# Instance norm over rows of 4096: two-pass statistics on both engines, with 4 MB tiles in six buffers and loads four ahead

## Chip, cores, metric

One core of one Trainium2 chip. The metric is device time in microseconds (us).

## The reference

```python
# x: (256, 256, 4096) float32, drawn from randn; eps = 1e-5
mean = np.mean(x, axis=2, keepdims=True)
var = np.var(x, axis=2, keepdims=True)
return ((x - mean) / np.sqrt(var + eps)).astype(np.float32)
```

That is 65,536 independent rows of 16 KB. 1.07 GB are read and 1.07 GB written.

## The kernel before

(Shortened.) Four rows on each of 128 partitions make a tile of 8 MB. Three such tiles fill the buffers. All transfers are issued by SP (the "queue" below), in one order.

```python
    P = 128
    K = 4
    BUFS = 3
    AHEAD = 2
    ...
    def load(i):
        x_tile = io.tile([P, K, d], mybir.dt.float32)
        nc.sync.dma_start(out=x_tile, in_=x_t[i])
        tiles[i] = x_tile

    def row(x_tile, r):
        ...
        for j in range(nsub):                       # nsub = 8, pieces of 512
            nc.vector.bn_stats(out=stats[:, j, :], in_=xr[:, r, j, :])
        nc.vector.bn_aggr(out=mv, in_=stats)
        nc.scalar.activation(out=rstd, in_=mv[:, 1:2], func=Sqrt, bias=eps_tile, scale=1.0)
        nc.vector.reciprocal(out=rstd, in_=rstd)
        nc.vector.scalar_tensor_tensor(out=nbias, ...)      # -mean * rstd
        nc.scalar.activation(out=x_tile[:, r, :], in_=x_tile[:, r, :],
                             func=Identity, bias=nbias, scale=rstd)

    def finish(i):
        x_tile = tiles.pop(i)
        for r in range(K):
            row(x_tile, r)
        nc.sync.dma_start(out=out_t[i], in_=x_tile)

    for i in range(AHEAD):
        load(i)
    for i in range(ntiles):
        finish(i)
        if i + AHEAD < ntiles:
            load(i + AHEAD)
```

## Time and profile before

| | before |
|---|---|
| time, median of 4 runs | 5018.83 us (5017.18 to 5019.74) |
| DMA engines' share on the data queue | 99.7% |
| VectorE, ScalarE busy | 53%, 42% |
| transfers, packet size | 256 of 8 MB, 65,536 B |
| instructions of VectorE, with waits | 5639 |

Read it from the DMA side. If the DMA share is at its top in every slice, busy shares of the compute engines say nothing about the time. What counts is GB/s, slice by slice (a page cuts the run into 40 equal slices), and the ends of the run. The lines are in the prediction.

### The profile page before, as it was taken

The numbers are of one execution on the slowest core, as the hardware profiler recorded it, in microseconds if no ns is written. First come the engines' busy times: TensorE is split into PE (matmuls) and PEld (weight loads), VectorE is DVE, ScalarE is ACT, GpSimd is POOL, SyncE is SP. The second block draws the span as 40 slices with busy tenths as digits, with TensorE's granted clock in tenths as the row PEclk, the third lists the DMA queues.
The fourth block names the chain that finished last, engine by engine and source line by source line (L and its number), as shares of the span: only waits on it lengthen the run. The fifth ranks groups of instructions, "written<-read, shape, count | busy, mean of one in ns | idle before, by whom it ended". The sixth has DMA issues, their size and how long they took to land.

```text
span 5018.0 us, 7844 instructions
## 1 busy us (share of the span) xinstructions
DVE 2667.3 (53%) x5633; ACT 2083.6 (42%) x1025; POOL 0.2 (0%) x4
## 2 busy tenths in 40 slices
DVE  5555455545555455554555545555455544555444
ACT  3444334443444334443344433444334443344433
POOL 0000000000000000000000000000000000000000
DMA  9999999999999999999999999999999999999998
GB/s 426 432 432 432 433 433 434 434 434 433 427 432 429 426 432 430 427 434 427 427 427 432 428 426 433 429 427 429 430 428 427 428 432 427 427 432 428 427 432 362
DMA packets 36925, 2148.00 MB, mean 428 GB/s; under 512 B 4096, under 2 KB 4096, under 8 KB 4096
## 3 DMA queue, kind: packets, MB, share of 16 engines
q1 hardware_dynamic: 36864, 2147.50, 99.7%
q14 instruction: 61, 0.50, 0.0%
HBM read 1073.74 MB, written 1073.74 MB: 428 GB/s over the span
## 4 chain that ended last, share of the span: by engine, by line
DVE 45%; another core or an unknown queue 43%; ACT 9%; DMA 1%; issue 1%; ACTq 0%
DVE stats L58 41%; ACT x_tile L76 9%; DVE mv L59 2%; DMA x_tile<-in_x_dram 1%; DVE rstd L67 1%; DVE nbias L68 1%; ACT rstd L60 1%; ACTq L60 0%
## 5 line engine op out<-in xcount | busy, mean ns | idle before, releaser
L58 DVE BATCH_NORM_STATS2 stats<-x_tile 128x6 f32<-128x512 f32 x4096 | 2506.3, 674 | 2228.2 <-DMA x_tile<-in_x_dram 2228.2
L76 ACT ACTIVATE x_tile<-x_tile,nbias,rstd 128x4096 f32<-128x4096 f32 x512 | 1945.7, 3800 | 403.5 <-DVE nbias L68 403.5
L60 ACT ACTIVATE rstd<-mv,eps_tile 128x1 f32<-128x1 f32 x512 | 148.8, 291 | 2508.5 <-DVE mv L59 2483.6
L59 DVE BATCH_NORM_AGGREGATE mv<-stats 128x2 f32<-128x48 f32 x512 | 183.7, 359 | 4.4
L67 DVE RECIPROCAL rstd<-rstd 128x1 f32<-128x1 f32 x512 | 74.8, 146 | 87.5 <-ACT rstd L60 87.3
L68 DVE SCALAR_TENSOR_TENSOR nbias<-mv,rstd 128x1 f32<-128x1 f32 x512 | 75.2, 147 | 4.3
L60 ACT ACT_TABLE_LOAD x1 | 1.3, 1283 | 0.7 <-PEq L112 0.7
L42 DVE MEMSET eps_tile<- 128x1 f32 x1 | 0.1, 59 | 0.8 <-PEq L112 0.8
L112 POOL MEMSET const-bfloat16-1.0<- 128x1 bf16 x1 | 0.1, 103 | 0.0
L112 POOL MEMSET const-uint8-127<- 128x1 uint8 x1 | 0.1, 102 | 0.0
L112 POOL MEMSET const-float32-0.0<- 128x1 f32 x1 | 0.1, 100 | 0.2 <-issue 0.2
L112 POOL MEMSET const-float32-1.0<- 128x1 f32 x1 | 0.1, 99 | 0.0
## 6 DMA issues: line engine op xcount, KB each, us to landing
x_tile<-in_x_dram SPq DMA_DIRECT2D x128, 52.3
out_dram<-x_tile SPq DMA_DIRECT2D x128, 33.3
```

The costliest lines, as they stand in the source:

```text
L42: nc.vector.memset(eps_tile, eps)
L58: nc.vector.bn_stats(out=stats[:, j, :], in_=xr[:, r, j, :])
L59: nc.vector.bn_aggr(out=mv, in_=stats)
L60: nc.scalar.activation(out=rstd, in_=mv[:, 1:2], func=mybir.ActivationFunctionType.Sqrt, bias=eps_tile, scale=1.0,)
L67: nc.vector.reciprocal(out=rstd, in_=rstd)
L68: nc.vector.scalar_tensor_tensor(out=nbias, in0=mv[:, 0:1], scalar=-1.0, in1=rstd, op0=mybir.AluOpType.mult, op1=mybir.AluOpType.mult,)
L76: nc.scalar.activation(out=x_tile[:, r, :], in_=x_tile[:, r, :], func=mybir.ActivationFunctionType.Identity, bias=nbias, scale=rstd,)
L112: nc = _bacc.Bacc("TRN2", target_bir_lowering=False, num_devices=1)
```

## The change

Its intent: fewer, longer instructions, shared by both engines, and smaller tiles of which more are in flight. The mean comes from a tensor_reduce in two stages, the squared deviations from a Square pass on ScalarE with an accumulator; one row is scaled by VectorE and the other by ScalarE. The same 24 MB of buffers hold six 4 MB tiles, and four loads are issued ahead. Instructions are kept in program order.

```diff
-    K = 4
-    BUFS = 3
-    AHEAD = 2
+    K = 2
+    BUFS = 6
+    AHEAD = 4
+    C = 64
...
-        for j in range(nsub):
-            nc.vector.bn_stats(out=stats[:, j, :], in_=xr[:, r, j, :])
-        nc.vector.bn_aggr(out=mv, in_=stats)
...
+        def mean(r):
+            row = x_tile[:, r, :].rearrange("p (c f) -> p c f", c=C)
+            keep(nc.vector.tensor_reduce(out=part[:, r, :], in_=row, axis=AX.X, op=ALU.add))
+            keep(nc.vector.tensor_reduce(out=nsum[:, c], in_=part[:, r, :], axis=AX.X, op=ALU.add, negate=True))
+            keep(nc.vector.tensor_scalar_mul(out=nmean[:, c], in0=nsum[:, c], scalar1=1.0 / d))
+        def square(r):
+            keep(nc.scalar.activation(out=junk, in_=x_tile[:, r, :], func=AF.Square,
+                                      bias=nmean[:, c], scale=1.0, accum_out=ss[:, c]))
+        def scales(c):          # Sqrt on ScalarE, reciprocal and nmean * rstd on VectorE
...
+        mean(0); square(0); mean(1)        # the loops of the diff, written out for k = 2
+        scales(row 0); square(1); scales(row 1)
+        apply_dve(1)                       # tensor_scalar on VectorE
+        apply_act(0)                       # Identity on ScalarE
...
     for i in range(AHEAD):
         load(i)
+    for i in range(last + 1):
+        compute(i)
+        store(i)
+        if i + AHEAD <= last:
             load(i + AHEAD)
```

(`junk` is a PSUM tile that takes the squares, which nobody reads.)

More of the change, by code (lines that the diff above doesn't have):

```diff
@@ L18 @@
     nc = tc.nc
+    keep = tc.keep_in_program_order
+    fp32 = mybir.dt.float32
+    AX = mybir.AxisListType
+    AF = mybir.ActivationFunctionType
+    ALU = mybir.AluOpType
     P = 128
-    K = 4
-    BUFS = 3
-    AHEAD = 2
+    K = 2
+    BUFS = 6
+    AHEAD = 4
+    C = 64
     x_flat = x.flatten_outer_dims()
@@ L26, with rows @@
     n, d = x_flat.shape
-    ntiles = n // (P * K)
-    assert n == ntiles * P * K
-    x_t = x_flat.rearrange("(t p k) d -> t p k d", p=P, k=K)
-    out_t = out_flat.rearrange("(t p k) d -> t p k d", p=P, k=K)
-    FMAX = nc.vector.BN_STATS_FMAX
-    nsub = d // FMAX
-    assert d == nsub * FMAX
+    assert n % (P * K) == 0 and d % C == 0
+    spans = [(t * P * K, K) for t in range(n // (P * K))]
+    last = len(spans) - 1
+    def rows(flat, span):
+        r0, k = span
+        return flat[r0 : r0 + P * k, :].rearrange("(p k) d -> p k d", k=k)
@@ L37 @@
     io = ctx.enter_context(tc.tile_pool(name="io", bufs=BUFS))
-    small = ctx.enter_context(tc.tile_pool(name="small", bufs=8))
+    small = ctx.enter_context(tc.tile_pool(name="small", bufs=4))
     singles = ctx.enter_context(tc.tile_pool(name="singles", bufs=1))
-    eps_tile = singles.tile([P, 1], mybir.dt.float32)
+    psum = ctx.enter_context(tc.tile_pool(name="psum", bufs=1, space=bass.MemoryType.PSUM))
+    eps_tile = singles.tile([P, 1], fp32)
     nc.vector.memset(eps_tile, eps)
+    junk = psum.tile([P, d], fp32)
@@ L44 @@
     tiles = {}
     def load(i):
-        x_tile = io.tile([P, K, d], mybir.dt.float32)
-        nc.sync.dma_start(out=x_tile, in_=x_t[i])
+        x_tile = io.tile([P, K, d], fp32)
+        keep(nc.sync.dma_start(out=x_tile[:, : spans[i][1], :], in_=rows(x_flat, spans[i])))
         tiles[i] = x_tile
-    def row(x_tile, r):
-        xr = x_tile.rearrange("p k (s f) -> p k s f", s=nsub)
-        stats = small.tile([P, nsub, 6], mybir.dt.float32)
-        mv = small.tile([P, 2], mybir.dt.float32)
-        rstd = small.tile([P, 1], mybir.dt.float32)
-        nbias = small.tile([P, 1], mybir.dt.float32)
-        for j in range(nsub):
-            nc.vector.bn_stats(out=stats[:, j, :], in_=xr[:, r, j, :])
-        nc.vector.bn_aggr(out=mv, in_=stats)
-        nc.scalar.activation(
-            out=rstd,
-            in_=mv[:, 1:2],
-            func=mybir.ActivationFunctionType.Sqrt,
-            bias=eps_tile,
-            scale=1.0,
-        )
-        nc.vector.reciprocal(out=rstd, in_=rstd)
-        nc.vector.scalar_tensor_tensor(
-            out=nbias,
-            in0=mv[:, 0:1],
-            scalar=-1.0,
-            in1=rstd,
-            op0=mybir.AluOpType.mult,
-            op1=mybir.AluOpType.mult,
-        )
-        nc.scalar.activation(
-            out=x_tile[:, r, :],
-            in_=x_tile[:, r, :],
-            func=mybir.ActivationFunctionType.Identity,
-            bias=nbias,
-            scale=rstd,
-        )
@@ L84, in finish, with compute, apply_dve, apply_act @@
-    def finish(i):
-        x_tile = tiles.pop(i)
-        for r in range(K):
-            row(x_tile, r)
-        nc.sync.dma_start(out=out_t[i], in_=x_tile)
+    def compute(i):
+        x_tile = tiles[i]
+        k = spans[i][1]
+        part = small.tile([P, K, C], fp32)
+        nsum = small.tile([P, K], fp32)
+        nmean = small.tile([P, K], fp32)
+        ss = small.tile([P, K], fp32)
+        std = small.tile([P, K], fp32)
+        rstd = small.tile([P, K], fp32)
+        nbias = small.tile([P, K], fp32)
+        def mean(r):
+            c = slice(r, r + 1)
+            row = x_tile[:, r, :].rearrange("p (c f) -> p c f", c=C)
[3 more added lines that the diff above has]
+        def square(r):
+            c = slice(r, r + 1)
+            keep(
+                nc.scalar.activation(
+                    out=junk, in_=x_tile[:, r, :], func=AF.Square, bias=nmean[:, c], scale=1.0, accum_out=ss[:, c]
+                )
+            )
+        def scales(c):
+            keep(nc.scalar.activation(out=std[:, c], in_=ss[:, c], func=AF.Sqrt, bias=eps_tile, scale=1.0 / d))
+            keep(nc.vector.reciprocal(out=rstd[:, c], in_=std[:, c]))
+            keep(nc.vector.tensor_mul(out=nbias[:, c], in0=nmean[:, c], in1=rstd[:, c]))
+        def apply_dve(r):
+            c = slice(r, r + 1)
+            row = x_tile[:, r, :]
+            keep(
+                nc.vector.tensor_scalar(
+                    out=row, in0=row, scalar1=rstd[:, c], scalar2=nbias[:, c], op0=ALU.mult, op1=ALU.add
+                )
+            )
+        def apply_act(r):
+            c = slice(r, r + 1)
+            row = x_tile[:, r, :]
+            keep(nc.scalar.activation(out=row, in_=row, func=AF.Identity, bias=nbias[:, c], scale=rstd[:, c]))
+        for r in range(k - 1):
+            mean(r)
+            square(r)
+        mean(k - 1)
+        scales(slice(0, k - 1))
+        square(k - 1)
+        for r in range(k - 2):
+            apply_dve(r)
+        scales(slice(k - 1, k))
+        apply_dve(k - 1)
+        apply_act(k - 2)
@@ L90, with store @@
+    def store(i):
+        keep(nc.sync.dma_start(out=rows(out_flat, spans[i]), in_=tiles.pop(i)[:, : spans[i][1], :]))
     for i in range(AHEAD):
         load(i)
-    for i in range(ntiles):
-        finish(i)
-        if i + AHEAD < ntiles:
+    for i in range(last + 1):
+        compute(i)
+        store(i)
+        if i + AHEAD <= last:
             load(i + AHEAD)
```

## The prediction

> **What bounds the kernel now.** I read the page from the top: busy shares, the slices, the queues.
>
> ```profile
> DVE 2667.3 (53%) x5633; ACT 2083.6 (42%) x1025; POOL 0.2 (0%) x4
> ...
> DMA  9999999999999999999999999999999999999998
> GB/s 426 432 432 432 433 433 434 434 434 433 427 432 429 426 432 430 427 434 427 427 427 432 428 426 433 429 427 429 430 428 427 428 432 427 427 432 428 427 432 362
> ...
> q1 hardware_dynamic: 36864, 2147.50, 99.7%
> ```
>
> Both compute engines are half idle; the DMA engines are full in every slice but the last. The bound is moving 2147.5 MB, and the change moves the same bytes. So the question is only what lies between 5018 us and the fastest these bytes can move. The trace's packet records give that: of the 32,768 data packets of 65,536 B, 95% took 2418 ns, which over 16 engines is 433.7 GB/s. At that pace the data takes 32768/16 x 2.418 = **4952 us**. All the change can win is 5018 - 4952 = 66 us, 1.3%. More than 2% faster is practically excluded.
>
> Where are these 66 us? Stages of the run (columns: stretch, length, busy time of the engines, clock, DMA share, GB/s), then the end:
>
> ```profile
> 200.00:1000.00 800.00, 435.61 (x919) 335.45 (x166) 0.00 (x0) 1.00 1.00 433
> 1000.00:2000.00 1000.00, 526.21 (x1112) 412.96 (x203) 0.00 (x0) 1.00 1.00 430
> 4000.00:4950.00 950.00, 510.65 (x1080) 398.91 (x197) 0.00 (x0) 1.00 1.00 429
> ```
>
> ```profile
> 4970.00:4978.00 8.00, 7.02 (x15) 0.31 (x2) 0.00 (x0) 1.00 0.93 401
> 4978.00:4986.00 8.00, 8.00 (x17) 7.00 (x3) 0.00 (x0) 1.00 0.25 107
> 4986.00:4996.40 10.40, 5.82 (x15) 8.96 (x5) 0.00 (x0) 1.00 0.01 6
> 4996.40:5016.00 19.60, 0.00 (x0) 0.00 (x0) 0.00 (x0) 1.00 0.99 428
> ```
>
> First: the rate falls from 433 to 429 GB/s after some 1000 us, though the DMA share stays 1.00. Over the 3950 us from 1000 to 4950 that is about 0.9%, 35 us. Second: before the last store the DMA stands nearly idle from 4978 to 4996.4 us (0.25 x 8 + 0.01 x 10.4 = 2 us of work in 18.4), because all other transfers are done and the last 8 MB tile is still being computed: **16 us**.
>
> For the first, the issuing queue:
>
> ```profile
> 4017.41 0.33 SPq L88 DMA_DIRECT2D out_dram<-x_tile  x1
> 4017.84 0.39 SPq L48 DMA_DIRECT2D x_tile<-in_x_dram  x1
> 4057.05 0.33 SPq L88 DMA_DIRECT2D out_dram<-x_tile  x1
> ```
>
> ```profile
> SPq L88 <- ACT x_tile L76: 3233.2, 128, 26.6
> SPq L88 <- DMA x_tile<-in_x_dram: 1631.0, 126, 20.5
> SPq L48 <- DMA out_dram<-x_tile: 22.3, 2, 12.2
> ```
>
> A store is issued every 39.2 us with the next load right behind it, and the queue waits for computation (L76), not for a free buffer. Lining the packets up end to start gives 16 chains, one per DMA engine (the records do not name the engine, so this is my reconstruction). Early on, a store waits 8 us in the queue before any engine starts it. From about 1150 us on, the engines that are ahead start it 1 to 2 us after its issue, while the slowest trails them by 12 us. The tile is complete only when the slowest has landed it; then come some 26 us of computation; then the store is issued, just as the fastest run dry. Before this point the slowest engine needed 38.90 us for a load and a store of 8 MB, the fast ones 38.65 to 38.70; afterwards all need 39.12. The excess appears as last packets of a transfer that take about 3 us instead of 2.418. So lookahead is just used up in this kernel.
>
> **What the Trainium skill says.** (1) "DMA: Bandwidth & Descriptors", section "Where 436 GB/s comes from": 16 ports give 435.2 GB/s. The packets' 433.7 agrees; no program change raises it. (2) "SBUF — State Buffer", section "The DMA setup-cost knee": about 2 us fixed cost per transfer. It doubles in number here, but the trace shows the next transfer's packets following with no gap, with 9 ns for the closing 4-byte packet, so in a filled queue it is hidden. (3) "VectorE: DVE Perf Modes", section "The perf-mode tier table": fp32 tensor_reduce runs at 1x (for 2048 elements its 1x row says 2293 ns), tensor_scalar at 2x (1227 ns). The kernel before has neither; its nearest, 674 ns for 512 elements of bn_stats, fits a 1x rate. (4) "ScalarE: Activation LUTs", section "What ACT_TABLE_LOAD costs": 280 + 0.833 ns per element, 93 ns more for a second per-row operand, so 3785 ns at 4096; the trace has 3800.
>
> **The change part by part.** Rows on which the costs rest:
>
> ```profile
> L58 DVE BATCH_NORM_STATS2 stats<-x_tile 128x6 f32<-128x512 f32 x4096 | 2506.3, 674 | 2228.2 <-DMA x_tile<-in_x_dram 2228.2
> L76 ACT ACTIVATE x_tile<-x_tile,nbias,rstd 128x4096 f32<-128x4096 f32 x512 | 1945.7, 3800 | 403.5 <-DVE nbias L68 403.5
> L60 ACT ACTIVATE rstd<-mv,eps_tile 128x1 f32<-128x1 f32 x512 | 148.8, 291 | 2508.5 <-DVE mv L59 2483.6
> ```
>
> *VectorE, per 4 MB tile (2 rows a partition).* Gone: 2 x (8 x 0.612 + 0.36 + 0.15 + 0.15) = 11.1 us. Added, as estimates scaled from the tier table's 2048-element figures: two reductions of 4096 elements at 4.43 us, each with a 64-element reduction and a small multiply (0.15 each, like the 146 ns reciprocal): 2 x 4.73 = 9.5; four tiny operations, 0.6; one tensor_scalar at 2x, 2.3. Sum 12.4 us, 3.2 ms in 256 tiles, 63%.
> *ScalarE, per tile.* Two Square passes with accumulator (3.8 plus perhaps 0.2), two Sqrt at 0.29, one apply at 3.8: 12.4 us against 8.2 before.
> *Path through a tile.* The engines now alternate: both means end at 9.5; the second Square at 13.6; Sqrt, reciprocal and multiply at 14.2; the VectorE apply at 16.5, when the next tile can begin; the ScalarE apply at 17.7. So a tile per **16.5 us**, latency **17.7 us**. The DMA needs 38.71/2 = 19.4 us for load and store of a tile. Compute fits, with 2.9 us to spare, though busier than now. All of it lies beside DMA work.
> *Lookahead.* Six 4 MB buffers hold the same 24 MB. When load i has landed, the filled queue holds three stores and three loads ahead of store i: 6 x 9.7 = 58 us. Store i is issued 18 us after landing, and load i+4 waits for store i-2, which lands some 31 us after, needed by 67. So the lag between engines may grow to about 35 us before anything runs dry; today 12 us is the end. At some 0.2 us per 16 MB over 128 such pairs the lag ends below 30 us. The loss of the 39.12 stage should not come.
> *Ends.* When the last load lands, three stores (29 us) are still queued, more than 17.7: the 16 us hole goes. At the start store 0 is ready at about 30 us, before four loads end at 41: no hole either.
> *Transfers.* 512 instead of 256, packets of 32 KB: if the pace per byte holds, 1.21 us each. Transfer ends double.
>
> Sum: the end is set by the slowest engine. 128 x 38.90 = 4979 us; its excess over 38.71 comes from fetch packets of 8 KB on the instruction queue (about 43 land on it, one per 128 instructions of VectorE), which halve with VectorE's instructions (5633 to some 2800): about -10. Doubled transfer ends: the other trailing engines, without such fetches, lost 0.1 us per pair against 38.71; doubled, another 0.1 x 128 = +13. Start and final receipt: 4, slow first packets: 4. Together **4990 us**, -0.6%.
>
> **Rivals.** (A) *Transfer ends cost by themselves*, and the 0.41 us per pair of the later stage is not lack of lookahead: then twice as many ends give 256 x 0.41 = 105 us instead of 52, hole gone: 5018 - 16 + 52 = 5054. For it: the excess sits in last packets, not in gaps. Against: under 1000 us the same ends cost a quarter of this. (B) *Compute becomes the bound*: 19.4 us per tile is passed if tensor_scalar ran at 1x and handovers cost 1 us, or if Square and Sqrt need different tables: a load is 1283 ns on the page, four per tile 5 us, so 21.6 us x 256 = 5500 us. Against: Identity and Sqrt already share one load; nothing in the trace settles Square. (C) *Everything is recovered*: 4952 + 8 = 4960. (D) *Nothing changes but the hole*: 5000.
>
> **Range and chances.** My sum and D lie at 4990 to 5000, C at 4960, A at 5054 with about one chance in eight. B has perhaps one in 25. Range 4960 to 5040; faster by over 2% 0.01, within 2% 0.95, slower 0.04.
>
> **What would show each step.** Right: GB/s near 433 to the end, with no fall after 1000 us; a last slice well over 362; no idle stretch before the last store; the queue waiting for landed stores rather than for computation; VectorE near 63%, ScalarE near 62%, one table load; reductions near 4.4 us, tensor_scalar near 2.3 us. Wrong: 32 KB packets over 1.21 us on average by more than 1% (A), or idle DMA in mid-run with tiles spaced over 19.4 us (B).

## More of the kernel before

```profile
q14 instruction: 61, 0.50, 0.0%
```

These are fetches of the program itself: 61 packets, half a megabyte, a share that rounds to nothing.

## The result

| | before | after |
|---|---|---|
| time, median of 4 runs | 5018.83 us | 4985.86 us (4984.90 to 4986.04) |
| ratio, 95% interval | | 0.9934 (0.9917 to 0.9952) |
| VectorE, ScalarE busy | 53%, 42% | 64%, 61% |
| transfers, packet size | 256, 65,536 B | 512, 32,768 B |

Ratios in this document are the mean time of one kernel's fast runs over the mean of the other's in the same rounds, so not quite the ratio of the quoted medians.

33 us were won, half of the 66 that there were. The page after, parts 1 to 3:

```profile
DVE 3189.2 (64%) x2817; ACT 3044.8 (61%) x1794; POOL 0.2 (0%) x4
...
GB/s 422 430 432 433 433 433 433 432 433 433 433 433 433 433 433 433 433 433 433 433 433 433 433 433 433 433 433 433 433 433 433 432 433 433 433 433 433 433 433 363
...
q1 hardware_dynamic: 73728, 2147.52, 99.9%
q14 instruction: 48, 0.39, 0.0%
```

Both compute engines work more, and the time is shorter. GB/s no longer falls in mid-run. The last slice is as poor as before, 363 against 362. The stages (columns as in the prediction: stretch, length, busy times, clock, DMA share, GB/s):

```profile
200.00:1000.00 800.00, 511.75 (x452) 487.32 (x287) 0.00 (x0) 1.00 1.00 433
1000.00:2000.00 1000.00, 643.97 (x567) 610.14 (x360) 0.00 (x0) 1.00 1.00 433
4000.00:4950.00 950.00, 607.92 (x540) 579.62 (x344) 0.00 (x0) 1.00 1.00 433
```

The waits of the queue have turned round. Before, a store waited for computation and hardly ever for a buffer. Now most of the waiting is a load that waits for a stored tile to land and leave its buffer free:

```profile
SPq L56 <- DMA out_dram<-x_tile: 2742.3, 246, 12.2
SPq L117 <- DVE x_tile L94: 1818.3, 256, 27.6
SPq L117 <- ACT x_tile L102: 212.5, 256, 1.0
```

The groups show what the new arithmetic costs:

```profile
L80 ACT ACTIVATE junk<-x_tile,nmean 128x4096 f32<-128x4096 f32 x512 | 1882.8, 3677 | 1887.4 <-DVE nmean L75 1887.4
L73 DVE TENSOR_REDUCE part<-x_tile 128x64 f32<-128x4096 f32 x512 | 2260.2, 4414 | 702.5 <-DMA x_tile<-in_x_dram 702.5
L102 ACT ACTIVATE x_tile<-x_tile,nbias,rstd 128x4096 f32<-128x4096 f32 x256 | 969.3, 3786 | 0.1
...
L94 DVE TENSOR_SCALAR x_tile<-x_tile,rstd,nbias 128x4096 f32<-128x4096 f32 x256 | 617.8, 2413 | 9.4
```

And the timeline of one tile, from its first reduction to the issue of its store:

```profile
2009.85 4.42 DVE L73 TENSOR_REDUCE part<-x_tile 128x64 f32<-128x4096 f32 x1 [2.71 <-DMA x_tile<-in_x_dram]
...
2027.36 0.34 SPq L117 DMA_DIRECT2D out_dram<-x_tile  x1
```

That is 17.5 us through a tile, and VectorE waits 2.71 us for the next load: compute keeps up.

Last, the end of the run:

```profile
4954.00:4962.00 8.00, 3.05 (x6) 7.79 (x4) 0.00 (x0) 1.00 0.17 74
4962.00:4972.60 10.60, 0.00 (x0) 0.00 (x0) 0.00 (x0) 1.00 0.93 399
4972.60:4983.00 10.40, 0.00 (x0) 0.00 (x0) 0.00 (x0) 1.00 0.07 28
```

In the last stretch a DMA share of 0.07 is one engine of 16: the packet records show a single packet in flight for 8.9 us, while 13 engines finished at 4972.6 and two more by 4973.9. In the first stretch three engines work and the rest wait for the last store, which is issued at 4961.97. So most engines still have a hole before the last store, of some 8 us, but the slowest one has none, and it sets the end. Before, all engines ended within 0.2 us of each other at 5016.7, because the last store made all of them start together.

### The profile page after: what moved, and what is told of

Same layout as the page of the kernel before. It is cut to its first block, busy times and chain, and to the rows that moved or that the text cites. A ratio compares the mean times of both kernels' runs of the same rounds, so it can differ in the third digit from the quotient of the medians.

```text
span 4983.9 us, 6181 instructions
## 1 busy us (share of the span) xinstructions
DVE 3189.2 (64%) x2817; ACT 3044.8 (61%) x1794; POOL 0.2 (0%) x4
## 2 busy tenths in 40 slices
DMA packets 73776, 2147.91 MB, mean 431 GB/s; under 512 B 8192, under 2 KB 8192, under 8 KB 8192
## 4 chain that ended last, share of the span: by engine, by line
DMA 63%; DVE 13%; another core or an unknown queue 12%; ACT 10%; issue 0%; SPq 0%; ACTq 0%
DMA x_tile<-in_x_dram 56%; DVE part L73 11%; DMA out_dram<-x_tile 8%; ACT junk L80 5%; ACT x_tile L102 5%; DVE nsum L74 1%; DVE nmean L75 0%; SPq L117 0%; DVE x_tile L94 0%; ACTq L156 0%; ACT std L86 0%; ACT L86 0%; DVE rstd L87 0%; DVE nbias L88 0%
## 5 line engine op out<-in xcount | busy, mean ns | idle before, releaser
L80 ACT ACTIVATE junk<-x_tile,nmean 128x4096 f32<-128x4096 f32 x512 | 1882.8, 3677 | 1887.4 <-DVE nmean L75 1887.4
L73 DVE TENSOR_REDUCE part<-x_tile 128x64 f32<-128x4096 f32 x512 | 2260.2, 4414 | 702.5 <-DMA x_tile<-in_x_dram 702.5
L102 ACT ACTIVATE x_tile<-x_tile,nbias,rstd 128x4096 f32<-128x4096 f32 x256 | 969.3, 3786 | 0.1
L87 DVE RECIPROCAL rstd<-std 128x1 f32<-128x1 f32 x512 | 81.3, 159 | 1006.5 <-ACT std L86 1006.5
L94 DVE TENSOR_SCALAR x_tile<-x_tile,rstd,nbias 128x4096 f32<-128x4096 f32 x256 | 617.8, 2413 | 9.4
L86 ACT ACTIVATE std<-ss,eps_tile 128x1 f32<-128x1 f32 x512 | 150.6, 294 | 16.5
L74 DVE TENSOR_REDUCE nsum<-part 128x1 f32<-128x64 f32 x512 | 112.7, 220 | 17.6
L80 ACT ACTIVATION_READ_ACCUMULATOR junk<-x_tile,nmean 128x1 f32 x512 | 95.5, 187 | 0.0
L88 DVE TENSOR_TENSOR nbias<-nmean,rstd 128x1 f32<-128x1 f32 x512 | 81.6, 159 | 17.5
L75 DVE TENSOR_SCALAR nmean<-nsum 128x1 f32<-128x1 f32 x512 | 78.7, 154 | 17.5
```

The source lines that it names most:

```text
L73: keep(nc.vector.tensor_reduce(out=part[:, r, :], in_=row, axis=AX.X, op=ALU.add))
L74: keep(nc.vector.tensor_reduce(out=nsum[:, c], in_=part[:, r, :], axis=AX.X, op=ALU.add, negate=True))
L75: keep(nc.vector.tensor_scalar_mul(out=nmean[:, c], in0=nsum[:, c], scalar1=1.0 / d))
L80: nc.scalar.activation(out=junk, in_=x_tile[:, r, :], func=AF.Square, bias=nmean[:, c], scale=1.0, accum_out=ss[:, c])
L86: keep(nc.scalar.activation(out=std[:, c], in_=ss[:, c], func=AF.Sqrt, bias=eps_tile, scale=1.0 / d))
L87: keep(nc.vector.reciprocal(out=rstd[:, c], in_=std[:, c]))
```

## The experiments

**The quantity behind them.** The packet records give start and length of each packet, not its engine. Each packet starts within some ns of the end of another, so they can be chained into 16 sequences. From these I read the **slack**: the time from the issue of a store until the first engine starts on it. It says how much work the fastest engine still had in its queue. It is a reconstruction, good to some 3 us (where engines lag by more than a transfer, the chains can be swapped). Experiments 1 to 4 ran on one chip, 5 to 7 on another, 8 to 11 on a third, 12 on a fourth, each beside the kernel before; its medians were 5018.95, 5024.45, 5018.26 and 5022.69 us.

| kernel | slack of a store, at us into the run | GB/s falls at about |
|---|---|---|
| before | 7.2 at 390, 3.7 at 777, 1.8 at 1164, then 0.8 to 1.8 | 1250 us, to 429 |
| after | 34.0 at 197, 27.9 at 2230, 19.5 at 4670 | never |

The slack of a load is read in the same way where it is named.

My theory: time is set by whether this slack lasts to the end of the run. It is one budget. Buffers and issue order fill it, the path through a tile takes from it, and the slowest DMA engine eats it up, because that engine carries instruction fetches besides its share of the data. Rivals: the arithmetic made the gain; the size of the transfers did; fetches are too small to matter.

### 1. Old arithmetic, new tiling

```diff
 (the changed kernel, with)
+        for j in range(nsub):
+            nc.vector.bn_stats(out=stats[:, j, :], in_=xr[:, r, j, :])
+        nc.vector.bn_aggr(out=mv, in_=stats)
+        ... (row as in the kernel before) in place of mean, square, scales and apply
```

(The statistics get 8 small buffers, and the order of the computing is not fixed, both as in the kernel before; loads and stores keep program order.)

> The old statistics (bn_stats, one apply on ScalarE) in the new tiling: 4 MB tiles, six buffers, loads four ahead, same order of transfers. Theory (the gain is lookahead, not arithmetic): nearly all of the gain stays; about 4993 us, some 7 us over the changed kernel, because VectorE's instructions double again (5633 instead of 3073 with waits, some 20 more fetch packets at about 0.5 us on the slowest DMA engine). GB/s flat at 433 to the end. Rival 1 (the long two-engine instructions made the gain): about 5018 us. Rival 2 (instruction fetches do not matter): 4986 us, equal to the changed kernel.

Measured: 5037.08 us median of 4 runs (5020.91 to 5061.15), ratio to before 1.0039 (1.0002 to 1.0075). My number was wrong by 44 us, and rival 1's by 19. Six buffers with four loads ahead are no gain at all with this arithmetic. The page shows how:

```profile
GB/s 422 431 433 434 432 433 434 434 432 433 433 433 432 433 434 433 432 433 434 433 432 433 434 433 432 433 434 432 433 433 424 418 414 411 418 416 414 410 415 308
...
q14 instruction: 66, 0.54, 0.0%
```

For 3780 us it runs at 433 GB/s, like the changed kernel. Then it falls, to 414, further than the kernel before ever did. The slack was 33.7 us at 603, 18.5 at 2230, 6.5 at 3857. So it is the same budget, filled higher and eaten faster than I had allowed: 8.6 us per 1000 us between 1010 and 3043 us, with 44 fetches in VectorE's stream over the run (5639 instructions, one fetch per 128), some 9 per 1000 us. I had reckoned half a microsecond for each; the slack shows about one.

The slack of a store stops at some 6 us here, and yet the rate falls. What has run out by then is the slack of a load: 9.4 us at 2966, 1.3 at 4087, 0.5 at 4857. With six buffers and four loads ahead, load i+4 needs the buffer of tile i-2, and so it waits until the slowest engine has stored that tile. The queue's waits from 4000 to 4900 us show this:

```profile
SPq L54 <- DMA out_dram<-x_tile: 656.1, 45, 15.8
SPq L81 <- ACT x_tile L76: 213.2, 44, 5.1
```

In the kernel before and in experiment 3 it is the store that is late, waiting for computation.

### 2. New arithmetic, old tiling

```diff
-    K = 2
-    BUFS = 6
-    AHEAD = 4
+    K = 4
+    BUFS = 3
+    AHEAD = 2
```

> The new arithmetic in the old tiling: 8 MB tiles, three buffers, two ahead. The path through such a tile is about 27.5 us (four means 19.2, last Square 3.9, Sqrt and scales 0.7, apply 3.8), hardly other than the 26 us of the old arithmetic. Theory: no gain; about 5025 us (5015 to 5040), with the hole before the last store, another of 8 us at the start (two loads in flight instead of three), and GB/s that falls to about 429 once lookahead is used up. Rival 1 (the arithmetic made the gain): 4986 us.

Measured: 5008.86 us (5006.68 to 5011.47), ratio to before 0.9979 (0.9964 to 0.9994). Neither number. So the arithmetic alone, in the old tiles, gives 10 of the 33 us. GB/s falls, but later:

```profile
GB/s 385 431 431 432 436 434 434 434 431 435 435 435 434 433 433 435 434 436 431 434 435 429 435 428 433 428 428 428 432 429 428 432 429 428 427 433 429 428 430 364
```

The slack starts as low as in the kernel before (6.9 us at 402) but reaches 1.8 only at 2141 us instead of 1164. VectorE has 2564 instructions here instead of 5639, so less than half the fetches in its stream (38 instead of 61 on the page, which counts all engines). I had forgotten them in this expectation.

### 3. and 4. Loads three and two ahead

```diff
-    AHEAD = 4
+    AHEAD = 3        # experiment 3; 2 in experiment 4
```

> The changed kernel with loads three tiles ahead instead of four, nothing else. A store then has 4 x 9.7 = 38.7 us from the landing of its load on a fast engine instead of 58; it is issued 18 us plus the lag of the slowest engine plus about 1.4 us after, so the lag may reach about 19 us, and it reaches about 20 only at the end of the run. Theory: 4986 us, within 5 us. Rival (each transfer of lookahead is worth something by itself): clearly over 4995 us.

> The changed kernel with loads two tiles ahead. Now a store has 19.4 us, and 18 us of computing plus 1.4 us of issue use all of it with no lag at all: every engine runs dry from the start. Two tiles take one store, one load (19.4 us), the lag between engines (2 to 3 us), 18 us of computing and 1.5 to 3 us of landing and issue: about 42 us instead of 38.7. Theory: about 5300 us (5150 to 5450), DMA share clearly under 1 throughout, idle time as gaps between transfers. Rival (lookahead is not what sets the pace): within 20 us of 4986.

Three ahead: 4989.3, 4989.5 and 5007.1 us in its fast runs (a fourth, 5149.85, was slow and is left out), ratio 0.9940 (0.9920 to 0.9960). The profiled run is the one of 5007.1: the slack of a store, 15.8 us at 402, is down to 1.4 at 4061 us, and the rate from 4000 to 4900 us is 426 GB/s instead of 433. It is just at the edge, as reckoned: two runs lie within my 5 us, one misses by 21. Why executions of one kernel differ so much here is not known.

Two ahead: 5145.22 us (5142.87 to 5147.56), ratio 1.0250 (1.0235 to 1.0265): slower, but by half of what I expected and just under my range. The sum was right in kind: a period of two tiles is 5143/128 = 40.2 us, and the parts are a load that lands 22.0 us after its issue (median), 0.4 from store to load, 17.5 us of computing, 39.9 in all. I had added the lag and the issue a second time; they are within the 22.0. One expectation was plainly wrong, that the DMA share would drop:

```profile
200.00:1000.00 800.00, 498.77 (x441) 475.73 (x281) 0.00 (x0) 1.00 1.00 419
1000.00:2000.00 1000.00, 623.50 (x551) 594.81 (x351) 0.00 (x0) 1.00 1.00 420
```

The share is 1.00 at 420 GB/s. The mean packet takes 1248 ns here and 1214 in the changed kernel. So shortage of lookahead hides in the lengths of packets. A DMA share of 1.00 does not say that the DMA is at its best; GB/s does.

### 5. Before, with a shorter path (a different computation)

```diff
-            nc.vector.bn_stats(out=stats[:, j, :], in_=xr[:, r, j, :])
+            nc.vector.bn_stats(out=stats[:, j, :], in_=xr[:, r, j, : FMAX // 2])
```

> The kernel before with bn_stats on half of each 512-element piece: WRONG RESULT ON PURPOSE. Same 256 transfers of 64 KB packets, same buffers, same number of instructions, so same fetches; only the path through a tile shrinks, from 26 to about 20 us. Theory: the lag between DMA engines may now grow to 18 us instead of 12 before a store is issued just in time, so GB/s stays at 433 until about 2200 us instead of 1000 and then falls to 429 or 430; the hole before the last store shrinks by about 6 us; together about 4998 us (4988 to 5006). Rival A (ends of 8 MB transfers or 64 KB packets cost by themselves): the fall comes at 1000 us as before, time 5008 to 5018.

Measured: 5011.75 us (5000.41 to 5012.63), ratio 0.9967 (0.9950 to 0.9983). (With data from randn, half a row gives statistics near enough to pass the comparison. It is still not what the reference computes.)

```profile
GB/s 403 434 434 433 432 431 434 434 434 434 435 433 434 432 435 434 428 432 428 428 428 429 432 428 431 430 429 427 432 428 429 428 430 430 429 427 433 429 432 366
```

The fall moves from about 1250 to about 2000 us, where 2200 was expected; the slack starts at 14.0 instead of 7.2 us (at some 390 us) and is 1.8 at 1942. Transfers, buffers and instructions are those of the kernel before. So the fall is not a matter of time passed or of the transfers' kind: six microseconds in the path put it off by some 750 us. The time, however, misses my range of 4988 to 5006 and lies in that of rival A, whose other sign, a fall at 1000 us, did not come. Against the kernel before on the same chip the gain is 13 us of the 20 expected.

### 6. and 8. Padding: many small instructions, or a single long one

```diff
         apply_act(k - 2)
+        for _ in range(11):
+            keep(nc.vector.memset(pad, 0.0))      # pad [P, 1]; experiment 6
+        keep(nc.vector.memset(pad, 0.0))          # pad [P, 1250]; experiment 8, instead of the 11
```

> The changed kernel with 11 one-element memsets per tile added on VectorE (59 ns each, about 0.7 us per tile, in its idle time; path lengthened by nothing that the queue of 58 us would show). 2816 more instructions are 22 more 8 KB fetch packets. Theory (what is left over 4960 is the lag of the DMA engine that carries VectorE's instruction fetches): about 4998 us (4992 to 5004). Rival (the left-over is start and end of the run): 4986 us, within 2.

> Control for the padding run: instead of 11 one-element memsets per tile (59 ns each, with the gaps between them 1.33 us per tile in that run's groups) one memset of 1250 elements, about 1.36 us per tile. VectorE's time and the path through a tile are lengthened as much as in the padding run (5066 us), but there are 256 more instructions instead of 2816, so 2 more fetch packets instead of 22. Theory (the fetches eat the lookahead): about 4988 us (4983 to 4995), GB/s 433 to the end. Rival (VectorE's added time or the longer path made the padding run slow): 5030 to 5070 us.

Eleven small ones: 5065.86 us (5030.91 to 5081.48), ratio to before 1.0072 (1.0032 to 1.0111): 80 us slower than the changed kernel, where I had expected 12. (These are different chips. By the ratios to the kernel before on each chip, 1.0072 against 0.9934, it is 1.4%, or 69 us.) One long one with nearly the same time on VectorE (1.10 us and a gap of 0.21, against 1.33 for the eleven): 4987.38 us (4985.16 to 4992.14), ratio 0.9939 (0.9924 to 0.9954), as expected. First the 11 small ones, then the long one:

```profile
GB/s 422 432 433 433 433 432 434 433 432 433 433 432 434 433 432 433 433 432 433 434 432 433 433 432 433 433 428 421 418 416 415 414 417 412 416 415 409 415 417 304
...
q14 instruction: 70, 0.57, 0.0%
```

```profile
GB/s 422 431 432 433 433 433 433 432 433 433 433 433 433 433 433 433 433 433 433 433 433 433 433 433 433 433 433 433 433 433 433 433 433 433 433 433 433 433 433 358
...
q14 instruction: 50, 0.41, 0.0%
```

This pair is the cleanest, though it ran on two chips (experiment 8 beside the changed kernel again, 4985.74 us). What differs is the number of instructions, and with it 20 packets of 8 KB out of 2148 MB. It is not these bytes that cost 70 to 80 us. They delay one DMA engine, the tile is complete only when that engine has landed its part, and after some 3300 us the slack is nearly gone (31.8 us at 604, 15.1 at 2230, 4.2 at 3453; that of a load is 2.9 at 3341 and 0.9 at 3721). From there all 16 engines lose 4%.

### 7. and 9. to 11. Fewer instructions, and how both parts add up

```diff
-    (tensor_reduce in two stages, scaled to the mean; Sqrt, reciprocal, nbias once per row)
+    for r in range(K):
+        tensor_reduce(out=nsum[:, r], in_=x_tile[:, r, :], axis=X, op=add, negate=True)    # one stage
+        activation(out=junk, in_=x_tile[:, r, :], func=Square, bias=nsum[:, r], scale=float(d),
+                   accum_out=ss[:, r])                              # (d * x - sum)^2
+    activation(out=std, in_=ss, func=Sqrt, bias=eps_tile, scale=1.0 / float(d) ** 3)       # both rows
+    reciprocal(out=rstd, in_=std)
+    scalar_tensor_tensor(out=nbias, in0=nsum, scalar=1.0 / d, in1=rstd, op0=mult, op1=mult)
     (row 1 on VectorE, row 0 on ScalarE, as in the changed kernel)
```

Experiment 9 is this lean kernel with AHEAD = 3; 10 is the changed kernel and 11 the lean one again, on one chip with 8 and 9.

> A correct kernel with the same tiling and fewer instructions: one tensor_reduce per row without the second stage, Square of (d x - sum) so that no mean is scaled, Sqrt, reciprocal and bias once per tile for both rows: VectorE 5 instead of 11 per tile, ScalarE one less. VectorE's fetches fall from 24 to about 12, so ScalarE's stream with about 16 to 18 becomes the longest. Theory: about 4981 us (4976 to 4984). Rival (fetches do not matter): 4986 us. If the reduction over 4096 elements in one go is slower than 4.4 us, or the path over 19 us, compute shows up instead.

> The lean kernel with loads three ahead instead of four. Do lag and lookahead add up as one budget? The changed kernel with three ahead used up its slack at about 4000 us (4998 us). The lean one loses slack more slowly (12 us over the run instead of 18 in the traces), so with some 10 us less of it at the start it should just reach the end. Theory: 4977 us (4973 to 4983), no fall of GB/s. Rival (three ahead is worse by itself): 4986 or more, as the changed kernel lost 12 us.

> The changed kernel as it is, beside the others on this chip, for a comparison on one chip: 4986 us (4983 to 4990).

> The lean kernel again, on the same chip as the changed kernel: 4975 us (4972 to 4979), so about 0.2% faster than the changed kernel. If on one chip both are within 3 us, its gain in the earlier job was the chip's.

| | median us (4 runs) | ratio to before |
|---|---|---|
| 7 lean | 4975.25 (4973.54 to 4975.46) | 0.9900 (0.9885 to 0.9915) |
| 9 lean, three ahead | 4977.70 (4975.73 to 4978.58) | 0.9918 (0.9903 to 0.9933) |
| 10 changed kernel again | 4985.74 (4984.81 to 4988.59) | 0.9935 (0.9921 to 0.9950) |
| 11 lean again | 4975.33 (4973.25 to 4977.36) | 0.9913 (0.9897 to 0.9930) |

The lean kernel is correct and the fastest correct one here: on one chip its four runs and those of the changed kernel do not overlap, and the medians are 10.4 us apart. I had at first expected 5 us, and 4976 to 4984 for the time; its fetches of both engines fell from 48 to 36 packets. Its page ends better, because the last engine trails less:

```profile
GB/s 421 433 433 432 433 434 434 433 433 434 433 433 433 434 433 432 433 434 433 432 433 434 433 433 433 434 433 432 433 434 433 433 433 434 432 433 433 434 432 395
...
q14 instruction: 36, 0.29, 0.0%
```

The slack falls only from 35.0 us at 1010 to 29.0 at 4670. And with it three ahead costs 2.4 us instead of the 3.5 to 21 us of experiment 3: where little is eaten, less need be stored. (Experiments 9 to 11 met their expectations; the 4998 us in that of experiment 9 is a median that includes the slow run of experiment 3, 4989.5 without it.) Lookahead and fetches are one budget.

### 12. Before, with few instructions (wrong result)

```diff
-        for j in range(nsub):
+        for j in range(1):
             nc.vector.bn_stats(out=stats[:, j, :], in_=xr[:, r, j, :])
-        nc.vector.bn_aggr(out=mv, in_=stats)
+        nc.vector.bn_aggr(out=mv, in_=stats[:, :1, :])
```

> The kernel before with statistics from one of the eight pieces of a row: WRONG RESULT ON PURPOSE. All transfers, 8 MB tiles, three buffers and the order of issue stay as before; only VectorE's instructions fall, from 5633 to 2049, and with them both the path through a tile (26 to about 19 us, now set by ScalarE) and the fetches (44 to 16). Theory: slack starts at about 15 us and loses some 13 us over the run, so it just lasts: GB/s 433 to the end, about 4980 us (4973 to 4990), as good as the 4 MB tiles. Rival (8 MB transfers, or 64 KB packets, are themselves what made the kernel before slow): the fall after 1000 us stays and the time is 5000 us or more.

Measured: 4969.79 us (4969.71 to 4970.55), ratio 0.9896 (0.9880 to 0.9913), 10 us under my number and 3 under my range. The result is wrong (relative error 0.05).

```profile
1000.00:2000.00 1000.00, 94.31 (x416) 409.91 (x208) 0.00 (x0) 1.00 1.00 434
4000.00:4900.00 900.00, 85.16 (x379) 371.80 (x188) 0.00 (x0) 1.00 1.00 434
```

With 8 MB tiles, 64 KB packets, three buffers and the old order of issue this has the lowest median of all (by the ratio it cannot be told from the lean kernel's 0.9900), and its rate never falls; the slack goes from 16.1 us at 392 to 4.0 at 4835. So neither small transfers nor six buffers are needed for the gain. (Path and fetches both fell here; this run does not part them, the pair 6 and 8 does.) Small tiles are one way to have slack enough, a short path with few instructions is another.

## Why the prediction was right

**The bound: right.** The median packet of the changed kernel takes 1213 ns for 32,768 B, 432 GB/s over 16 engines. (Of the packets before, 91% took exactly 2418 ns, not 95%; the median is the same.) No kernel here came under 4969 us; the floor reckoned from the packets was 4952.

**The lost lookahead: right, and the main step.** The fall from 433 to 429 is gone, and the queue waits for landed stores. Experiments 1, 3, 5, 6 and 12 each move the fall by moving the slack. The prediction allowed a lag between engines of 35 us and expected it below 30; by the chains the slowest trailed the fastest by 16 us at 4600 us.

**The hole before the last store: wrong for most engines.** The last slice was to be "well over 362"; it is 363. The slowest engine has no hole. The other 13 to 15 have one of 8 us and then finish early. What the last slice showed before was a common hole; what it shows after is one engine trailing. The step that failed is "three stores (29 us) are still queued, more than 17.7": it left out the lag of the slowest engine, which completes the tile. No loads come behind the last four stores, so from one to the next the slack falls by a transfer: 18.5, 8.8, -0.8 and -10.5 us. The lean kernel, with fewer fetches, comes with 28.6 and ends at -0.2; its last slice is 395.

**Compute: right.** 17.5 us through a tile (17.7 predicted), 19.35 - 2.71 = 16.6 us per tile at most (16.5), the reduction 4414 ns (4430), tensor_scalar 2413 (2300), VectorE 64%, ScalarE 61% (63 and 62). One small miss: two table loads instead of one, both before the first tile is done, none later, so that case of rival B is out.

**The slowest engine's sum: right in total, with terms mis-sized that cancel in part.** The prediction took 4979 us for the slowest engine, -10 for fewer fetches, +13 for twice as many transfer ends, 8 for start and end. The slowest engine ended at 4982.8 us. By the chains, the fast engines needed 19.362 us for load and store of 4 MB (1000 to 4600 us), against 38.638 for 8 MB in the kernel before (250 to 1000 us) and in experiment 12: 256 x 19.362 = 4957 against 128 x 38.638 = 4946. So twice as many packets and ends cost 11 us, near the 13 taken, but little of it sits in the ends: after the first 600 us the last packet of a transfer takes 1214 ns on average and any other 1213. Rival A, which wanted 52 us more, is out by this and by experiment 12. Two other terms were off. The pace without fetches, 128 x 38.71 = 4955 in the prediction, was 4946. And the fetches cost more than I took, about 0.75 us each instead of 0.57 (24 us for 43): slack lost in the changed kernel was 32.7 - 19.5 = 13.2 us from 1011 to 4670 us, with some 18 fetches for VectorE in that time (24 over the whole run). In the sum: predicted were 4955 + 14 + 13 + 8 = 4990; measured are 4946 + 18 + 11 = 4975, which leaves 11 of the 4986 for start and end. That the total fits within 4 us is in part luck.

The packet records show what a fetch costs. Its packet takes 309 ns. But in the changed kernel, in all 46 cases after 200 us, the data packet that starts as the fetch ends takes longer than 1213 ns too, by 119 to 573 ns. On the chain that carries the longest row of them (18, some 200 us apart) fetch and delay come to 0.77 us on average, and this chain trails the fastest by 5.0 us at 1000 and 12.8 at 3000 us, the chains in the middle by 1 to 3. So that the engine with the fetches is the slowest is seen, not only argued. Between 1000 and 3000 us the slack lost per fetch is 1.0 in experiments 1 and 6; what more is lost there is not known. Over long stretches it is 0.7 to 1.0 in the kernels here. It is reckoned on VectorE's stream alone, and ScalarE has fetches too, so this is no fixed price.

**What the prediction had not seen** is how near the edge it stood. It took lookahead for a matter of buffers and path, and the fetches for 10 us. With the old arithmetic in the new tiling, its own reasoning gave 4993 us and the chip 5037. The halved number of instructions was not a small correction to the change but a condition of its success.

**What stays open.** Once the slack is gone, the lost time appears as last packets of a transfer that take about 3 us instead of 2.4, also on engines whose queue is not empty then. And the rate falls to 429 with 8 MB tiles but to 414 with 4 MB tiles when four loads are ahead (experiments 1 and 6). What the queue waits for differs, a store for computation in the first case, a load for a stored tile in the second; why the second costs more, no run here tells. The Trainium skill, "DMA: Bandwidth & Descriptors", section "Anatomy of one DMA — SWDGE (gpsimd) path", says of transfers issued by GpSimd (here SP issues them) that a fixed cost of about 2 us is mostly the wait for the last byte to be confirmed. A wait of that kind, hidden while the queue is full, would fit, but this is argued, not shown.

## What to carry to other kernels

In a kernel that is bound by transfers, look at GB/s over the run and not only at the DMA share: a fall in mid-run at a share of 1.00 is lookahead that has run out. Count what fills it (loads in flight, issue order) and what eats it: the path from landing to store, the wait of a load for a stored tile's buffer, and the lag of the slowest DMA engine, which grows with the number of instructions in the longest stream. When tiles or buffers are changed, check also how many instructions there are; eleven tiny instructions per tile in VectorE's idle time cost this kernel 70 to 80 us, and one long one of the same duration nothing clear.

## What the Trainium skill lacked or had wrong

- "Runtime: NRT & Kernel Launch", section "Instruction fetch mechanics", calls the cost of a refill "mostly hidden". In a kernel at full DMA rate it is not: 22 more packets (70 instead of 48 on the page) went with 70 to 80 us (experiments 6 and 8). It also gives blocks of 16 KiB and 256 instructions; the trace has packets of 8192 B, about one per 128 instructions (61 packets for 7844).
- "SBUF — State Buffer", section "The DMA setup-cost knee", advises the largest single transfer. In a filled queue 4 MB and 8 MB ran alike, 433 and 434 GB/s (experiments 7 and 12). The page does not say that size ceases to matter there, nor what a queue that runs short costs (420 GB/s with two loads ahead).
- No page that I read tells that the 16 DMA engines drift apart over a run, or how much lookahead that takes (slack 34.0 us at the start of the changed kernel, 19.5 near its end).
- "VectorE: DVE Perf Modes", section "The perf-mode tier table", gives no time for tensor_reduce, only 1x; the 2293 ns that the prediction scaled is the table's figure for tensor_tensor at 1x. The estimate of 4430 ns held for 4096 elements, measured 4414; that for tensor_scalar, 2294, was 5% short of the measured 2413.
